# Tying sums of weight blocks to the split that precedes them, in a hybrid decoder step on one core

## The chip, the cores and the metric

One core of one Trainium2 chip runs the whole step: one prompt of 512 tokens with 16 meta tokens ahead of it, and eight sample tokens. The metric is the device time of one execution in microseconds. The kernel before took 2041.84 us, the median of three runs (2037.86 to 2042.74).

## What is computed

One layer: input projection, windowed attention beside causal pooling, output projection, layer norm, a SwiGLU block, layer norm. The change lies in the SwiGLU block, which is

```python
mix = jnp.einsum('bte,ed->btd', jnp.concatenate([attn_out, pool_out], -1), w_o)
h1 = layer_norm(DEEPNORM_ALPHA * h + mix, ln1_g, ln1_b)
a = jax.nn.silu(jnp.einsum('btd,df->btf', h1, w_gate)) * jnp.einsum('btd,df->btf', h1, w_up)
ff = jnp.einsum('btf,fd->btd', a, w_down)
return layer_norm(DEEPNORM_ALPHA * h1 + ff, ln2_g, ln2_b)
```

with D_MODEL = 2048 and D_FF = 5632, for 520 tokens (512 prompt, 8 sample) in float32.

## The kernel before

**Three matmuls per weight block.** Every float32 weight block s is split (L181 to L187) into a rounded part wh, written by ScalarE (L185, a cast), and a remainder wl = s - wh, written by VectorE (L186). I call these two instructions the cast and the split's low part. `products` (L189) then issues three matmuls per block of 128 rows: wh by the high part of the activations (L192), wh by their low part (L193), wl by their high part (L195). So TensorE can begin a product when the cast is there, and meets the low part at its third matmul.

**Seven products in the place of eight.** Gate, up and most of down are computed as 2 x 2 block products with seven multiplications each. Four of the seven multiply a sum or difference of weight blocks, which VectorE makes in place: product 7 of (0,0) - (1,0), product 6 of (1,1) - (1,0), product 5 of (1,0) + (0,0), product 3 of (0,1) - (1,0), where the later ones read what the earlier ones wrote to (1,0). Products 1, 2 and 4 multiply a loaded block. "Sum" below means one of these four instructions: L930 for gate and up (128 x 1024), L1160 for down (128 x 640).

**Gate and up.** One set is one column tile of gate or of up: seven products, each with two halves of four blocks (`Set`, L915). 22 gate sets and 22 up sets alternate (g0, u0, g1, ...). The wh and wl tiles of a half turn in rings of five; the loaded weights turn in a ring of five tiles. VectorE also adds the products' PSUM banks into the outputs (L985, L991, L998, L1001, L1004, L1007) and stages the activations for the next part (L1024 to L1054). In the bank names p1_g11 is the bank of gate set 11 that products 1, 6, 5 and 3 fill, p7_g11 that of 7 and 4, p2_g11 that of 2. The first two sets of each kind and the ten after them have product 1 (some product 2 too) done ahead; I call them the filled sets. Of these g1, g2, g3, g4 and g6 and the up sets beside them take part in what follows.

**Down.** 32 pairs (chunk c of 4, column pair j of 8), each a generator with seven products of five blocks, so 7 x 5 x 3 = 105 matmuls (`column_pair`, L1141). Its PSUM tile is tri{c}_{j}: bank 0 for products 7 and 4, bank 1 for 2, bank 2 for 1, 6, 5 and 3. The outer loop (L1197) interleaves two pairs: product 1 of a pair is written ahead of product 3 of the pair before. wh and wl turn in rings of four. The weights of a pair are two tiles of 640 KB in a ring of eight, so four pairs fit; `load_w` (L1126) for pair x+3 stands behind the last product of pair x-1, whose buffers it takes. VectorE adds the banks into the accumulators: L1167 behind product 7, L1172 behind 6, L1177 behind 5, L1180 behind 3.

**Who sets the order.** The program is written down in the order of the code, and a scheduler then lays out each engine's queue by priorities and by its own model of time, keeping only the dependencies. Casts, splits and sums get a raised priority (`tc.high_priority`), so a sum can be pulled far ahead of where the code has it. Each engine runs its queue in order.

Of the kernel before, what the change touches and what calls it, by code (L numbers as in the profile page):

```python
# [7 lines left out]
F32 = mybir.dt.float32  # L8
# [58 lines left out]
def hybrid_step(ctx, tc, xin, w_in, w_o, w_g, w_u, w_d, w_pool, par_d, cst_d, ident_d, ln2gb, kct_d, vc_d, hist_d,  # L67
                ck_d, cv_d, sp_d, yp, ys, nkp, nvp, npp, nks, nvs, nps):
    nc = tc.nc
# [68 lines left out]
    prio = [0]  # L138
# [42 lines left out]
    def split(s, name, lo=None):  # L181

        wh, wl = [sp[0].tile(list(s.shape), F32R, tag=t, bufs=sp[1]) for t in ("wh", "wl")]
        with tc.high_priority(prio[0]):
            nc.scalar.copy(wh, s)  # L185
            (lo or nc.vector).tensor_sub(wl, s, wh.bitcast(F32))  # L186
        return wh, wl  # L187

    def products(out, wh, wl, hi, lo, first, last, onto=False):  # L189

        for j, o in enumerate(out):
            nc.tensor.matmul(o, wh, hi[j], start=first, stop=False, skip_group_check=onto)  # L192
            nc.tensor.matmul(o, wh, lo[j], start=False, stop=False, skip_group_check=onto)  # L193
        for j, o in enumerate(out):
            nc.tensor.matmul(o, wl, hi[j], start=False, stop=last, skip_group_check=onto)  # L195

    def full_block(src, name, out, hi, lo, low=None, apart=False):


        def mm(w, g, js):  # L200
            for kk in range(4):
                k = g * 4 + kk
                sl = slice(kk * P, (kk + 1) * P)
                products([out[j] for j in js], w[0][:, sl], w[1][:, sl], [hi(k)[j] for j in js], [lo(k)[j] for j in js],
                         k == 0, k == KT - 1)

        js = list(range(len(out)))
        ws = []
        for h in range(2):
            raw = load_raw(src[:, h * 1024:(h + 1) * 1024], f"{name}_{h}")  # L210
            for g in range(2):
                ws.append(split(raw[:, g * 512:(g + 1) * 512], f"{name}_{h}{g}", low))
                mm(ws[-1], 2 * h + g, js[:1] if apart else js)
        if apart:
            for g in range(4):
                mm(ws[g], g, js[1:])
# [27 lines left out]
    with ExitStack() as sa:  # L244
# [149 lines left out]
        def kv_weights(g, blocks):  # L394
            kvw.setdefault(g, []).extend(split(kvr[g, i // 2][:, i % 2 * 512:i % 2 * 512 + 512], f"kv{g}{i}")
                                         for i in blocks)
# [254 lines left out]
        def pool_group(g, apart=False):  # L651

            raw = load_raw(w_pool[:, g * 512:(g + 1) * 512], f"pool{g}")
            wph, wpl = split(raw, f"pool{g}")
            kbs = [8 + 2 * g + m for m in range(2)]
            for kb in kbs:
                mixf[kb] = row_tile(f"mixf{kb}")
            for hs in ((0,), (1,)) if apart else ((0, 1),):
                for m, kb in enumerate(kbs):
                    out = [mm_tile(f"pm{g}_{m}_{h}")[:, :HN] for h in hs]  # L660
                    for k in range(2):
                        c = k * 256 + m * P
                        products(out, wph[:, c:c + P], wpl[:, c:c + P], [dd[2 * g + k][0][:, HALF[h]] for h in hs],
                                 [dd[2 * g + k][1][:, HALF[h]] for h in hs], k == 0, k == 1)
                    for h, o in zip(hs, out):
                        nc.scalar.activation(mixf[kb][:, HALF[h]], o, AF.Copy, scale=par[:, PSC + kb - 8:PSC + kb - 7])
                yield
# [132 lines left out]
    def slot(name, shape=(2, HN), at=None):  # L800
        return gp.tile([P, *shape], F32R, tag="g", name=name, bufs=NG, at=at)
# [3 lines left out]
    for h in range(2):  # L805
        for k2 in range(KT // 2):
            mh[h].append(slot(f"mh{h}_{k2}"))
            ml[h].append(slot(f"ml{h}_{k2}"))
            for kk in range(2):
                s = mixf[2 * k2 + kk][:, HALF[h]]  # L810
# [104 lines left out]
    class Set:  # L915
# [10 lines left out]
            return self.raw[r, c]  # L926

        def s(self, t, a, b, op):
            with tc.high_priority(prio[0]):
                op(self.q(*t), self.q(*a), self.q(*b))  # L930
            return self.q(*t)

        def prod(self, n, bk, first=True):
# [207 lines left out]
    def column_pair(c, j):  # L1141

        A = {(r, b): wd[c, j, r, b] for r in range(2) for b in range(2)}
        tri = ps.tile([P, 3, 512], F32, tag="tri", name=f"tri{c}_{j}", bufs=2)[:, :, :HN]
        ga, de, al = [tri[:, i, :] for i in range(3)]
        ac = acc4[j]
        if c == 0:
            for r in range(2):
                h = ac[:, 2 * r:2 * r + 2, :]
                nc.scalar.activation(h, h, AF.Copy, scale=ALPHA)  # L1150

        def prod(n, bk, src, first=True):
            wh, wl = split(src, f"d{c}_{j}_{n}")
            for k in range(KP):
                hi, lo = ops[c][n][k][:, 0, :], ops[c][n][k][:, 1, :]
                products([bk], wh[:, k, :], wl[:, k, :], [hi], [lo], k == 0 and first, k == KP - 1, True)

        def add(t, a, b, op):
            with tc.high_priority(prio[0]):
                op(A[t], A[a], A[b])  # L1160
            return A[t]


        prod(1, al, A[0, 0])
        yield
        prod(7, ga, add((1, 0), (0, 0), (1, 0), nc.vector.tensor_sub))
        nc.vector.tensor_add(ac[:, 1:3, :], ac[:, 1:3, :], tri[:, 0::2, :])  # L1167
        yield
        prod(2, de, A[0, 1])
        yield  # L1170
        prod(6, al, add((1, 0), (1, 1), (1, 0), nc.vector.tensor_sub), False)
        nc.vector.tensor_add(ac[:, 0, :], ac[:, 0, :], al)  # L1172
        yield
        prod(4, ga, A[1, 1], False)
        yield
        prod(5, al, add((0, 0), (1, 0), (0, 0), nc.vector.tensor_add), False)
        nc.vector.tensor_add(ac[:, 0:2, :], ac[:, 0:2, :], tri[:, 0::2, :])  # L1177
        yield
        prod(3, al, add((0, 1), (0, 1), (1, 0), nc.vector.tensor_sub), False)
        nc.vector.tensor_add(ac[:, 2:4, :], ac[:, 2:4, :], tri[:, 1:3, :])  # L1180
        yield
# [15 lines left out]
    for x, (c, j) in enumerate(pairs[2:], 2):  # L1197
# [5 lines left out]
        for i in range(5):  # L1203
# [7 lines left out]
            elif j == 0 and i == 0:  # L1211

                ah, al_ = [], []
                for f in range(2 * len(PLAIN)):
                    t = slot(f"af{f}", (NTOK,), 16 + f).bitcast(F32)
# [173 lines left out]
```

## Time and profile before

| | before |
|---|---|
| median of 3 runs | 2041.84 us |
| the profiled execution | 2042.2 us |
| its span, first to last instruction | 2040.4 us |
| TensorE busy | 1939.2 us, 95% |
| VectorE busy | 1534.8 us, 75% |
| ScalarE busy | 946.6 us, 46% |
| mean DMA rate | 156 GB/s |
| mean granted TensorE clock | 0.982 |

The span leaves out 1.8 us around the instructions. Gate and up fill most of the stretch from 600 to 1469 us, down that from 1469 to about 1966 us, of which 1500 to 1930 us holds nothing else; the rest is input projection, attention and output projection ahead, and the last products of two plain column tiles and the last layer norm behind. A row of the windows view gives the busy time of each engine in a stretch, in microseconds, then the granted clock, the DMA share and the rate. A row of the waits view says who waited for whom, how long in all, how often, and the longest.

### The profile page before, as it was taken

How to read it: one execution, taken by the hardware profiler on the slowest of the kernel's cores; microseconds unless marked ns; L12 is line 12 of the kernel's file. 1: busy time of each engine (PE TensorE's matmuls, PEld its weight loads, DVE VectorE, ACT ScalarE, POOL GpSimd, SP SyncE). 2: the span in 40 equal slices, each digit the busy share in tenths (PEclk: the TensorE clock that was granted, in tenths of full speed). 3: DMA queues.
4: the chain of work that ended last, by engine and by line, in shares of the span. 5: the costliest groups of instructions: out<-in, count | busy, mean ns of one | idle time of the engine just before them, and what ended most of it. 6: DMA issues, size and time to landing. Idle time of an engine off the chain costs nothing.

```text
span 2040.4 us, 39488 instructions
## 1 busy us (share of the span) xinstructions
PE 1939.2 (95%) x15571; PEld 1896.8 (93%) x15571; DVE 1534.8 (75%) x2730; ACT 946.6 (46%) x1805; POOL 2.5 (0%) x8
## 2 busy tenths in 40 slices
PE   8999999999999999999999999999998888888995
PEld 8999999999989999999999999999998888888895
DVE  6666667666678889888888888888876666666678
ACT  6643436446464444555555555555443333333331
POOL 0000000000000000000000000000000000000000
PEclk9999999999999999999999999999999999999998
DMA  8722223656564555444445444445785445353232
GB/s 261 232 84 78 73 79 101 205 183 209 170 195 151 169 182 172 143 164 135 152 146 166 135 162 144 158 136 186 254 293 193 139 149 192 125 183 111 71 94 84
DMA packets 144986, 319.27 MB, mean 156 GB/s; under 512 B 14160, under 2 KB 65944, under 8 KB 144696
## 3 DMA queue, kind: packets, MB, share of 16 engines
q1 hardware_dynamic: 143680, 314.65, 46.9%
q8 instruction: 122, 2.00, 0.4%
q10 hardware_dynamic: 1120, 2.10, 0.3%
q14 instruction: 64, 0.52, 0.1%
HBM read 265.20 MB, written 54.03 MB: 156 GB/s over the span
## 4 chain that ended last, share of the span: by engine, by line
PE 71%; DVE 12%; DMA 11%; issue 3%; ACT 2%; DVEq 0%; SPq 0%; ACTq 0%
DMA fr<-in_w_d_dram 6%; PE p_u L195 6%; PE p_u L192 6%; PE p_u L193 6%; DVE rr L186 5%; PE p_g L192 5%; PE p_g L193 5%; PE p_g L195 5%; PE tri L192 4%; PE tri L195 4%; PE tri L193 4%; PE o L192 3%; PE o L195 3%; PE o L193 3%; DMA fr<-in_w_u_dram 2%
## 5 line engine op out<-in xcount | busy, mean ns | idle before, releaser
L185 ACT CAST rr<-fr 128x512 fp32r<-128x512 f32 (+1 forms) x1056 | 664.7, 643 | 837.9 <-PE tri L193 226.1
L186 DVE TENSOR_TENSOR rr<-fr,rr 128x512 fp32r<-128x512 f32 (+1 forms) x1056 | 736.1, 717 | 210.4 <-ACT rr L185 204.5
L930 DVE TENSOR_TENSOR fr<-fr 128x1024 f32<-128x1024 f32 x176 | 215.3, 1224 | 63.2 <-DMA fr<-in_w_g_dram 34.3
L195 PE MATMUL tri<-rr 128*128 128x260 f32 x696 | 205.9, 296 | 37.4 <-DVE rr L186 36.3
L192 PE MATMUL p_g<-rr 128*128 128x260 f32 x800 | 227.1, 285 | 5.2 <-DVE fr L1001 5.2
L192 PE MATMUL p_u<-rr 128*128 128x260 f32 x800 | 226.2, 284 | 2.2 <-ACT rr L185 1.3
L195 PE MATMUL p_g<-rr 128*128 128x260 f32 x800 | 222.2, 282 | 1.3 <-DVE rr L186 1.3
L195 PE MATMUL p_u<-rr 128*128 128x260 f32 x800 | 222.3, 282 | 0.0
L193 PE MATMUL p_u<-rr 128*128 128x260 f32 x768 | 215.9, 282 | 0.0
L193 PE MATMUL p_g<-rr 128*128 128x260 f32 x768 | 215.8, 282 | 0.0
L192 PE MATMUL tri<-rr 128*128 128x260 f32 x696 | 204.4, 294 | 4.9 <-DVE fr L1177 1.8
L193 PE MATMUL tri<-rr 128*128 128x260 f32 x696 | 202.7, 291 | 0.0
L1160 DVE TENSOR_TENSOR fr<-fr 128x640 f32<-128x640 f32 x128 | 104.8, 822 | 102.5 <-DMA fr<-in_w_d_dram 102.3
L195 PEld LDWEIGHTS tri<-rr 128*128 128x128 f32 x696 | 137.7, 198 | 43.2 <-DVE rr L186 43.2
L192 PEld LDWEIGHTS p_g<-rr 128*128 128x128 f32 x800 | 150.6, 188 | 7.7 <-DVE fr L1001 7.3
L192 PEld LDWEIGHTS p_u<-rr 128*128 128x128 f32 x800 | 150.7, 188 | 3.6 <-ACT rr L185 1.9
L195 PEld LDWEIGHTS p_g<-rr 128*128 128x128 f32 x800 | 149.5, 189 | 1.5 <-DVE rr L186 1.5
L195 PEld LDWEIGHTS p_u<-rr 128*128 128x128 f32 x800 | 149.6, 189 | 0.0
L192 PE MATMUL o<-rr 128*128 128x260 f32 x512 | 146.0, 286 | 0.3 <-ACT rr L185 0.3
L193 PEld LDWEIGHTS p_u<-rr 128*128 128x128 f32 x768 | 144.3, 188 | 0.0
L193 PEld LDWEIGHTS p_g<-rr 128*128 128x128 f32 x768 | 144.3, 188 | 0.0
L195 PE MATMUL o<-rr 128*128 128x260 f32 x512 | 143.9, 283 | 0.2 <-DVE rr L186 0.2
(300 smaller groups left out, 4770.7 us busy)
## 6 DMA issues: line engine op xcount, KB each, us to landing
fr<-in_w_g_dram SPq DMA_DIRECT2D x95, 512.0 KB
fr<-in_w_u_dram SPq DMA_DIRECT2D x95, 512.0 KB
fr<-in_w_d_dram SPq DMA_DIRECT2D x64, 640.0 KB
t_d<-fr SPq DMA_DIRECT2D x140, 260.0 KB
fr<-in_w_o_dram SPq DMA_DIRECT2D x64, 512.0 KB
fr<-in_w_in_dram SPq DMA_DIRECT2D x46, 512.0 KB
rr<-t_d SPq DMA_DIRECT2D x87, 260.0 KB
mid_b<-t_d SPq DMA_DIRECT2D x53, 260.0 KB
```

The source lines that it names most:

```text
L185: nc.scalar.copy(wh, s)
L186: (lo or nc.vector).tensor_sub(wl, s, wh.bitcast(F32))
L192: nc.tensor.matmul(o, wh, hi[j], start=first, stop=False, skip_group_check=onto)
L193: nc.tensor.matmul(o, wh, lo[j], start=False, stop=False, skip_group_check=onto)
L195: nc.tensor.matmul(o, wl, hi[j], start=False, stop=last, skip_group_check=onto)
L930: op(self.q(*t), self.q(*a), self.q(*b))
L1160: op(A[t], A[a], A[b])
```

## The change

Each sum now carries a dependency on the low part of the split that was written down last before it, in the order of the code. The dependency is of order alone (no semaphore: both run on VectorE): it tells the scheduler that the sum may not stand ahead of that split in VectorE's queue. Nothing is computed otherwise, and the number of instructions of each kind stays.

```diff
         with tc.high_priority(prio[0]):
             nc.scalar.copy(wh, s)
-            (lo or nc.vector).tensor_sub(wl, s, wh.bitcast(F32))
+            last_lo[0] = (lo or nc.vector).tensor_sub(wl, s, wh.bitcast(F32)).ins
         return wh, wl
+
+    last_lo = [None]
+
+    def weight_sum(op, *args):
+
+        with tc.high_priority(prio[0]):
+            i = op(*args).ins
+        tc.add_manual_dep(i, last_lo[0].name, mybir.DependencyInfo(mybir.DependencyClass.NoSync,
+                                                                   mybir.DependencyReason.DATA), reason="sum")
...
         def s(self, t, a, b, op):
-            with tc.high_priority(prio[0]):
-                op(self.q(*t), self.q(*a), self.q(*b))
+            weight_sum(op, self.q(*t), self.q(*a), self.q(*b))
             return self.q(*t)
...
         def add(t, a, b, op):
-            with tc.high_priority(prio[0]):
-                op(A[t], A[a], A[b])
+            weight_sum(op, A[t], A[a], A[b])
             return A[t]
```

The nine new lines move the line numbers: a sum is L194 in the changed kernel, the matmuls are L201, L202 and L204, and the additions of banks stand 7 or 8 lines further down. The orders below are those of the queues; they hold no times.

VectorE's queue in down, from the addition behind product 6 of pair (2,2) on (tri2_2 is its PSUM tile, tri2_3 the next pair's). Before:

```order
L1172 TENSOR_TENSOR fr_60<-fr_60,tri2_2_18244 128x260
L186 TENSOR_TENSOR rr_61<-fr_60,rr_61 128x640
L1160 TENSOR_TENSOR fr_60<-fr_60 128x5x128
L186 TENSOR_TENSOR rr_61<-fr_60,rr_61 128x640
L1177 TENSOR_TENSOR fr_60<-fr_60,tri2_2_18244 128x520
L1160 TENSOR_TENSOR fr_60<-fr_60 128x5x128
L186 TENSOR_TENSOR rr_61<-fr_60,rr_61 128x640
L1160 TENSOR_TENSOR fr_60<-fr_60 128x5x128
L1167 TENSOR_TENSOR fr_60<-fr_60,tri2_3_18377 128x520
L1160 TENSOR_TENSOR fr_60<-fr_60 128x5x128
L186 TENSOR_TENSOR rr_61<-fr_60,rr_61 128x640
L1180 TENSOR_TENSOR fr_60<-fr_60,tri2_2_18244 128x520
```

Counted off against the code, the first L186 is the low part of product 3 of (2,2), and the first L1160 is the sum of product 7 of pair (2,5), three pairs ahead; the three others are the sums of products 6, 5 and 3 of (2,3). With the change the same place reads:

```order
L1179 TENSOR_TENSOR fr_60<-fr_60,tri2_2_18244 128x260
L186 TENSOR_TENSOR rr_61<-fr_60,rr_61 128x640 x2
L194 TENSOR_TENSOR fr_60<-fr_60 128x5x128
L186 TENSOR_TENSOR rr_61<-fr_60,rr_61 128x640
L1184 TENSOR_TENSOR fr_60<-fr_60,tri2_2_18244 128x520
L186 TENSOR_TENSOR rr_61<-fr_60,rr_61 128x640
L194 TENSOR_TENSOR fr_60<-fr_60 128x5x128
L1174 TENSOR_TENSOR fr_60<-fr_60,tri2_3_18377 128x520
L186 TENSOR_TENSOR rr_61<-fr_60,rr_61 128x640
L1187 TENSOR_TENSOR fr_60<-fr_60,tri2_2_18244 128x520
```

The first L194 is now the sum of product 7 of (2,3), the next pair, right ahead of its own split; no sum stands more than a few instructions ahead of the split that reads it. TensorE's order of products is the same in both from the third pair on.

VectorE's queue in gate set 11, from the addition of product 2 on. Before:

```order
L998 TENSOR_TENSOR fr_60<-p2_g11_10474,fr_60 128x260
L186 TENSOR_TENSOR rr_61<-fr_60,rr_61 128x512 x2
L930 TENSOR_TENSOR fr_60<-fr_60 128x1024
L1001 TENSOR_TENSOR fr_60<-fr_60,p1_g11_10373 128x260
L186 TENSOR_TENSOR rr_61<-fr_60,rr_61 128x512 x2
L1004 TENSOR_TENSOR fr_60<-fr_60,p7_g11_10404 128x260
```

With the change:

```order
L1006 TENSOR_TENSOR fr_60<-p2_g11_10474,fr_60 128x260
L186 TENSOR_TENSOR rr_61<-fr_60,rr_61 128x512 x2
L1009 TENSOR_TENSOR fr_60<-fr_60,p1_g11_10373 128x260
L186 TENSOR_TENSOR rr_61<-fr_60,rr_61 128x512 x2
L194 TENSOR_TENSOR fr_60<-fr_60 128x1024
L1012 TENSOR_TENSOR fr_60<-fr_60,p7_g11_10404 128x260
```

The sum is that of product 7 of the up set that follows (u11). It has moved from ahead of the addition of bank p1_g11 (L1001, now L1009) to behind it and behind the two splits of product 1 of u11.

TensorE's queue in gate set 3, one of the filled ones, where product 4 begins (bank p7_g3). Before:

```order
L192 MATMUL p2_g3_7456<-mid_b_3870,rr_61 128x260
L193 MATMUL p2_g3_7456<-mid_b_3870,rr_61 128x260
L195 MATMUL p2_g3_7456<-mid_b_3870,rr_61 128x260
L192 MATMUL p7_g3_7385<-rr_61 128x260
L193 MATMUL p7_g3_7385<-rr_61 128x260
L192 MATMUL p1_g3_7384<-rr_61 128x260
```

With the change:

```order
L201 MATMUL p1_g3_7384<-rr_61 128x260
L202 MATMUL p1_g3_7384<-rr_61 128x260
L204 MATMUL p1_g3_7384<-rr_61 128x260
L201 MATMUL p7_g3_7385<-rr_61 128x260
L202 MATMUL p7_g3_7385<-rr_61 128x260
L201 MATMUL p1_g3_7384<-rr_61 128x260
```

Before, product 2 (bank p2_g3) is the last ahead of product 4; now it is the second half of product 6 (bank p1_g3), and product 2 has come earlier. Gate sets 1, 2, 3, 4 and 6 are so.

## The prediction

> **What bounds the kernel now.** I read the page first, then windows by stage, then the waits of the stage that stands out, then the timeline of one of its pairs, then windows of 1 us for the clock. Page:
>
> ```profile
> span 2040.4 us, 39488 instructions
> PE 1939.2 (95%) x15571; PEld 1896.8 (93%) x15571; DVE 1534.8 (75%) x2730; ACT 946.6 (46%) x1805; POOL 2.5 (0%) x8
> ```
>
> TensorE is busy 95% of the span, but that is a mean over stages. The windows view for gate and up, for 10 us of the change to down, for all of down, and for 22 whole pairs in it (start and length, then busy time of PE, PEld, DVE, ACT and POOL, granted clock, DMA share, GB/s):
>
> ```profile
> 600.00:1469.00 869.00, 856.86 (x7075) 851.26 (x7073) 733.51 (x1156) 451.19 (x844) 0.00 (x0) 1.00 0.49 160
> 1480.00:1490.00 10.00, 10.00 (x86) 10.00 (x85) 5.71 (x8) 4.57 (x7) 0.00 (x0) 1.00 0.89 350
> 1500.00:1930.00 430.00, 376.49 (x2869) 366.55 (x2870) 290.43 (x414) 144.56 (x203) 0.00 (x0) 0.95 0.47 156
> 1555.89:1907.64 351.75, 304.50 (x2311) 296.06 (x2311) 234.63 (x335) 113.63 (x158) 0.00 (x0) 0.95 0.45 150
> ```
>
> Gate and up have TensorE busy for 98.6% of the time at full clock: little to win. Down has it idle for 53.5 of 430 us, at a granted clock of 0.95, with every other engine and the DMA further from full: there a wait is the bound. Who waits for whom in down (sum, times, longest):
>
> ```profile
> DVE fr L1160 <- DMA fr<-in_w_d_dram: 102.3, 24, 5.6
> PE tri L195 <- DVE rr L186: 41.0, 22, 2.8
> PE tri L192 <- DVE fr L1177: 7.3, 4, 3.5
> PE tri L192 <- DVE fr L1167: 4.2, 4, 1.8
> ```
>
> VectorE waits 24 times, once per pair, for a weight transfer, and only at the sum; TensorE waits 22 times for a low part. The timelines of one pair (start, length, instruction, and in brackets the idle time ahead of it with its releaser), sorted by time, show that it is one event:
>
> ```profile
> 1740.01 3.21 SPq L1133 DMA_DIRECT2D fr<-in_w_d_dram  x2
> 1741.27 0.73 ACT L185 CAST rr<-fr 128x640 fp32r<-128x640 f32 x1 [1.01 <-PE tri L193]
> 1742.04 0.83 DVE L186 TENSOR_TENSOR rr<-fr,rr 128x640 fp32r<-128x640 f32 x1 [0.21 <-ACT rr L185]
> 1742.98 0.28 PE L192 MATMUL tri<-rr 128*128 128x260 f32 x1
> 1746.56 0.28 PE L192 MATMUL tri<-rr 128*128 128x260 f32 x1
> 1746.96 0.82 DVE L1160 TENSOR_TENSOR fr<-fr 128x640 f32<-128x640 f32 x1 [4.10 <-DMA fr<-in_w_d_dram]
> 1747.70 0.82 DVE L186 TENSOR_TENSOR rr<-fr,rr 128x640 fp32r<-128x640 f32 x1
> 1748.57 0.38 PE L195 MATMUL tri<-rr 128*128 128x260 f32 x1 [1.62 <-DVE rr L186]
> ```
>
> The low part at 1742.04 ends at 1742.87 and is the last reader of two weight tiles; their next load moves from 1742.89 to 1746.87 (the chain of waits has it as its own step, below). The sum, next in VectorE's queue, needs that load, so VectorE stands for 4.10 us. Behind it is queued the low part of 1747.70, which starts as the sum ends, so its cast was ready; TensorE, at 1748.57, needs that one. Load, sum and low part are 3.98 + 0.82 + 0.82 us in a row against TensorE's lead. The queue in the section on the change says the same: the sum is that of the pair three ahead, and nothing needs it yet.
>
> **Part 1: the wait in down goes.** With the change the sum of product 7 of a pair stands right ahead of its own split, some three pairs after its load could begin. Two of the chain's rows give the length of the 22 pairs, and one the load:
>
> ```profile
> 1555.89 0.39 PE tri L195
> 1742.89 3.98 DMA fr<-in_w_d_dram
> 1907.64 0.39 PE tri L195
> ```
>
> Between the two matmuls, both right behind a stall, lie 351.75 us and 22 x 105 = 2310 matmuls, the 2311 of the window: 15.99 us a pair. Undisturbed matmuls, from 1742.98 to 1746.56, are 30 in 3.58 us: 0.1193 us each. So 2310 x 0.1193 = 275.6 us, 12.53 a pair, and 76.1 us are lost, 3.46 a pair: 47.3 as idle time (351.75 - 304.50), the other 28.9 at a lowered clock. Both go if the stall does: **-76.1**. The load has then 2 to 3 pairs, over 25 us, for its 4.
>
> Outside of these 22 pairs down idles 53.5 - 47.3 = 6.2 us more, partly behind the additions L1177 and L1167 (rows above), some of which were late behind a sum. I take half: **-3.1**.
>
> What is late next? VectorE's work for a pair, by groups of one shape between 600 and 1930 us (busy, mean ns | idle before):
>
> ```profile
> L186 DVE TENSOR_TENSOR rr<-fr,rr 128x640 fp32r<-128x640 f32 x210 | 169.0, 822 | 34.2 <-ACT rr L185 33.0 <-PE tri L195 0.3
> L1160 DVE TENSOR_TENSOR fr<-fr 128x640 f32<-128x640 f32 x122 | 99.9, 822 | 102.5 <-DMA fr<-in_w_d_dram 102.3
> L1167 DVE TENSOR_TENSOR fr<-fr,tri 128x520 f32<-128x520 f32 x30 | 20.8, 693 | 1.2 <-PE tri L195 1.2
> L1172 DVE TENSOR_TENSOR fr<-fr,tri 128x260 f32<-128x260 f32 x30 | 12.7, 425 | 5.6 <-PE tri L195 5.6
> ```
>
> Seven low parts, four sums, three additions of 520 columns (L1167, and L1177 and L1180 at the same price) and one of 260: 11 x 0.822 + 3 x 0.693 + 0.425 = 11.55 us, against TensorE's 12.53. VectorE fits, but at 92%, so order decides. A ring of four wh and wl lets a cast begin when the product four splits back has ended, and where TensorE then has just one product (15 matmuls, 1.79 us) ahead of it and meets the low part two matmuls later (0.24), the chain has 2.03 us. It takes, from the rows of the pair above, about 0.05 to the cast (as from the low part's end, 1748.52, to its matmul), 0.77 from its start to the low part's (1741.27 to 1742.04), and 0.87 from the start of the low part to its matmul (1747.70 to 1748.57): 1.7. The slack of 0.33 us is less than one more VectorE instruction. Followed by hand through the new queue, product 7 and product 1 of the next pair are the two with so short a lead in each pair, and both pass, since the sum of product 7 is done about 0.6 us before its buffer comes free. For jitter I take 0.2 us a pair over 27 pairs, an estimate between nothing and the 2 x (0.82 - 0.33) = 1.0 that one VectorE instruction in the way of both would cost: **+5.4**, with ends 0 and 27.
>
> Where does the clock come from? Windows of 1 us around the stall ahead of the one above (the digits behind the five engines are the clock, DMA share, GB/s):
>
> ```profile
> 1731.00:1732.00 1.00, 0.00 (x0) 0.00 (x0) 1.00 (x2) 0.00 (x0) 0.00 (x0) 1.00 0.63 243
> 1733.00:1734.00 1.00, 1.00 (x10) 1.00 (x10) 1.00 (x3) 0.01 (x1) 0.00 (x0) 0.95 0.00 0
> 1734.00:1735.00 1.00, 1.00 (x6) 1.00 (x6) 1.00 (x2) 0.72 (x1) 0.00 (x0) 0.50 0.00 0
> 1736.00:1737.00 1.00, 1.00 (x7) 1.00 (x7) 1.00 (x2) 0.21 (x1) 0.00 (x0) 0.50 0.00 0
> ```
>
> TensorE stands still through 1731 to 1732, works again, and gets half the clock from 1734 to 1737. At 1480 to 1490, with no idle time and twice the DMA traffic, the clock is 1.00. So I count the lowered clock as a consequence of the stalls. The Trainium skill, page "TensorE: Matmul & The Clock Gate", section "HAM oscillation — how this bites in real kernels", sets its rule at TensorE-idle gaps longer than about 3.4 us; the longest wait for a low part here is 2.8, so by it these stalls would not lower the clock, the cause would be another and would stay, as in the first rival. The trace disagrees: the 0.50 comes within 3 us of such a stall.
>
> **Part 2: gate and up.** TensorE's waits there:
>
> ```profile
> PE p_g L192 <- DVE fr L1001: 5.2, 8, 1.7
> PE p_u L195 <- DVE rr L186: 2.7, 4, 0.7
> PE p_g L195 <- DVE rr L186: 1.3, 1, 1.3
> PE p_u L192 <- ACT rr L185: 1.3, 3, 0.7
> PE p_u L192 <- DVE fr L1001: 0.9, 2, 0.5
> ```
>
> Together 11.4 us. Set 11 (timelines) shows the main kind:
>
> ```profile
> 994.76 1.23 DVE L930 TENSOR_TENSOR fr<-fr 128x1024 f32<-128x1024 f32 x1 [2.00 <-DMA fr<-in_w_u_dram]
> 995.90 0.42 DVE L1001 TENSOR_TENSOR fr<-fr,p_g 128x260 f32<-128x260 f32 x1
> 996.37 0.39 PE L192 MATMUL p_g<-rr 128*128 128x260 f32 x1 [0.61 <-DVE fr L1001]
> ```
>
> The sum waits for the up set's weights, and the addition that frees a PSUM bank waits behind it. The change puts the addition first, and takes sums from between casts and low parts: **-11.4**. In return gate sets 1, 2, 3, 4 and 6 get TensorE's new order (the second half of product 6 directly ahead of product 4), and the cast for product 4 takes the buffer that this half has just left. With no lead TensorE waits for a whole cast:
>
> ```profile
> L185 ACT CAST rr<-fr 128x512 fp32r<-128x512 f32 x586 | 353.2, 619 | 321.1 <-PE p_u L193 118.9 <-PE p_g L193 84.1 <-DVE fr L930 76.5
> ```
>
> 0.62 and about 0.05 on each side, say 0.75 us, five times: **+3.8** (0 if the other engines run later than I think). The stage nets -7.6; its ends are -11.4 and, if the old stalls only move, +3.8.
>
> **Sum**, against the profiled execution of 2042.2 us (the span and 1.8 around it; 0.4 above the median): 2042.2 - 76.1 - 3.1 + 5.4 - 7.6 = **1960.8, forecast 1961 us**. No instruction is added or removed, and no queue other than VectorE's and a few places of TensorE's and ScalarE's is moved.
>
> **The rivals.**
> *The clock stays low.* If down's 0.95 were due to load and not to stalls, 0.05 x 430 = 21.5 us would remain: 1982. Against it are the 1.00 at 1480 to 1490 and the 0.50 behind a stall. Chance 0.08.
> *The slack is eaten.* The upper end of the residue: a low part late by one VectorE instruction at both tight products of each pair, 27 us in the place of 5.4: 1982; with the clock lowered by it too, 2004. For it speaks VectorE's 92%; against it the order, walked by hand. Chance 0.20.
> *The wait only moves.* The first split that reads the load waits in the sum's place, and only gate and up gain: 2042.2 - 7.6 = 2035. Against it: the load is issued pairs ahead and takes 4 us, with DMA at 0.47. Chance 0.04.
> *The lost lead, slower.* Sums made early were ready when their cast came. Now the sum waits for the preceding low part, that one for its cast, that one for TensorE to free a buffer. If a sum ends after its buffer is free, sum, cast and low part stand in a row: 0.82 + 0.05 + 0.77 + 0.87 = 2.51 us of stall where nothing was hidden before. Over 3.46 / 2.51 = 1.4 such sums per pair the change loses; with two it is 2042.2 + (5.0 - 3.46) x 27 - 7.6 = 2076. Against it: the sum with the shortest lead is done 0.6 us early. Chance 0.05.
>
> **Numbers.** The forecast has 0.63, and gives 1961. Its own ends are 1948 (no residue, no new wait in gate and up, all of the 6.2) and 1974 (twice the residue, nothing won in gate and up). To reach 8 in 10 the range takes in the rivals at 1982 and, with the clock, 2004; below, the 2 us by which runs of a kernel scatter: 1946 to 2004. A difference of 0.3%, 6 us, is about what a measurement of this kernel can tell from no change. Faster 0.92, same 0.03 (a wait that only moves, with a little less gain than priced), slower 0.05.
>
> **What would show it.** Right: sums that wait for w_d loads almost gone (102.3 us before); 22 pairs of down in about 280 us at clock 1.00 with TensorE busy 98% and more; VectorE near 90% there; the waits for L1009 (the old L1001) gone; five waits of about 0.75 us for casts in gate sets 1 to 4 and 6. Wrong: pairs of over 13.2 us with TensorE waiting for low parts that follow a sum directly (lost lead, or slack eaten), a clock under 0.98 in down without stalls, or a load that the split now waits for.

## The result and the profile after

| | before | changed |
|---|---|---|
| median | 2041.94 us (4 runs) | 1976.12 us (4 runs, 1975.06 to 1978.68) |
| ratio | | 0.9683, 95% interval 0.9667 to 0.9700 |
| the profiled execution's span | 2040.4 us | 1974.6 us |
| mean granted clock | 0.982 | 0.987 |

The kernel is 65.8 us faster; the forecast was 81 us, 1961, and the measured time lies inside its range. The page of the changed kernel:

```profile
span 1974.6 us, 39350 instructions
PE 1916.5 (97%) x15571; PEld 1881.8 (95%) x15571; DVE 1545.2 (78%) x2730; ACT 936.6 (47%) x1805; POOL 2.5 (0%) x8
```

The page hides that the stages went opposite ways. The windows view shows it, for the first 300 us of gate and up and for 370 us of down. First the kernel before, then the changed one:

```profile
600.00:900.00 300.00, 293.01 (x2397) 289.68 (x2396) 261.45 (x426) 148.72 (x272) 0.00 (x0) 1.00 0.50 163
1530.00:1900.00 370.00, 321.44 (x2448) 312.40 (x2447) 248.61 (x355) 119.99 (x167) 0.00 (x0) 0.95 0.46 152
```

```profile
600.00:900.00 300.00, 278.38 (x2179) 271.46 (x2178) 244.22 (x393) 133.97 (x248) 0.00 (x0) 0.97 0.47 152
900.00:1400.00 500.00, 500.00 (x4172) 500.00 (x4172) 424.65 (x655) 263.01 (x510) 0.00 (x0) 1.00 0.46 149
1530.00:1900.00 370.00, 368.21 (x3061) 367.27 (x3060) 314.15 (x445) 151.70 (x215) 0.00 (x0) 1.00 0.52 178
```

The counts of matmuls in a stretch of fixed length are the shortest way to read such a change. Down gets 3061 in the place of 2448, TensorE 99.5% busy at full clock: 370 / 3061 x 105 = 12.69 us a pair, where I had forecast 12.53 and 0.2. The later sets of gate and up (900 to 1400 us) have no idle time left, and 4172 matmuls where the kernel before has 4128. But between 600 and 900 us, where the filled sets are, 218 matmuls fewer are done, 26 us at 0.1193. TensorE's waits of the changed kernel there, and those left in down (1530 to 1900 us):

```profile
PE p_g L201 <- ACT rr L185: 7.4, 10, 1.7
PE p_g L201 <- DVE fr L999: 6.7, 5, 1.4
PE p_g L201 <- DVE fr L1009: 4.1, 3, 2.9
PE p_g L204 <- DVE rr L186: 2.8, 6, 1.1
```

```profile
PE tri L204 <- DVE rr L186: 1.2, 1, 1.2
PE tri L201 <- DVE fr L1179: 0.6, 1, 0.6
```

In down two waits are left, 1.8 us together, where there had been one per pair. In the filled sets TensorE waits for casts and for additions of banks. Two of the prediction's signs did not come: VectorE is at 85% in down (314.15 of 370 us), not near 90, and three waits for L1009 (the old L1001) are left, though all ahead of 900 us.

### The profile page after: what moved, and what is told of

It is laid out like the page before. It is cut to its first block, busy times and chain, and to the rows that moved or that the text cites. A ratio compares the mean times of both kernels' runs of the same rounds, so it can differ in the third digit from the quotient of the medians.

```text
span 1974.6 us, 39350 instructions
## 1 busy us (share of the span) xinstructions
PE 1916.5 (97%) x15571; PEld 1881.8 (95%) x15571; DVE 1545.2 (78%) x2730; ACT 936.6 (47%) x1805; POOL 2.5 (0%) x8
## 4 chain that ended last, share of the span: by engine, by line
PE 58%; DVE 5%; DMA 2%; issue 1%; ACT 1%; DVEq 0%; ACTq 0%; SPq 0%
PE tri L201 7%; PE tri L204 7%; PE tri L202 7%; PE p_u L201 6%; PE p_u L202 6%; PE p_u L204 6%; PE p_g L201 6%; PE p_g L204 6%; PE p_g L202 6%; DMA fr<-in_w_g_dram 2%; DVE fr L194 2%; DVE rr L186 1%; PE d L204 1%; DMA t_d<-fr 1%; PE d L202 1%
## 5 line engine op out<-in xcount | busy, mean ns | idle before, releaser
L185 ACT CAST rr<-fr 128x512 fp32r<-128x512 f32 (+1 forms) x1056 | 655.6, 643 | 849.7 <-DVE fr L194 289.0
L186 DVE TENSOR_TENSOR rr<-fr,rr 128x512 fp32r<-128x512 f32 (+1 forms) x1056 | 733.4, 716 | 265.6 <-ACT rr L185 253.7
L194 DVE TENSOR_TENSOR fr<-fr 128x1024 f32<-128x1024 f32 (+1 forms) x304 | 319.3, 1050 | 37.3 <-DMA fr<-in_w_g_dram 21.7
L201 PE MATMUL p_g<-rr 128*128 128x260 f32 x800 | 231.2, 290 | 15.9 <-DVE fr L999 6.7
L204 PE MATMUL p_g<-rr 128*128 128x260 f32 x800 | 225.8, 287 | 1.1 <-DVE rr L186 1.1
L201 PE MATMUL p_u<-rr 128*128 128x260 f32 x800 | 225.5, 283 | 0.0
L204 PE MATMUL p_u<-rr 128*128 128x260 f32 x800 | 222.0, 282 | 0.0
L202 PE MATMUL p_g<-rr 128*128 128x260 f32 x768 | 219.6, 287 | 0.0
L202 PE MATMUL p_u<-rr 128*128 128x260 f32 x768 | 216.0, 282 | 0.0
L204 PE MATMUL tri<-rr 128*128 128x260 f32 x696 | 196.8, 283 | 1.2 <-DVE rr L186 1.2
L201 PE MATMUL tri<-rr 128*128 128x260 f32 x696 | 197.1, 283 | 0.8 <-ACT rr L185 0.8
L202 PE MATMUL tri<-rr 128*128 128x260 f32 x696 | 196.7, 283 | 0.0
L201 PEld LDWEIGHTS p_g<-rr 128*128 128x128 f32 x800 | 154.2, 193 | 19.9 <-DVE fr L999 7.7
L204 PEld LDWEIGHTS p_g<-rr 128*128 128x128 f32 x800 | 153.3, 193 | 1.4 <-DVE rr L186 1.3
L201 PEld LDWEIGHTS p_u<-rr 128*128 128x128 f32 x800 | 150.6, 188 | 0.0
L204 PEld LDWEIGHTS p_u<-rr 128*128 128x128 f32 x800 | 149.7, 189 | 0.0
L202 PEld LDWEIGHTS p_g<-rr 128*128 128x128 f32 x768 | 148.0, 193 | 0.0
L201 PE MATMUL o<-rr 128*128 128x260 f32 x512 | 146.0, 286 | 0.3 <-ACT rr L185 0.3
L202 PEld LDWEIGHTS p_u<-rr 128*128 128x128 f32 x768 | 144.3, 188 | 0.0
L204 PE MATMUL o<-rr 128*128 128x260 f32 x512 | 143.9, 283 | 0.2 <-DVE rr L186 0.2
L202 PE MATMUL o<-rr 128*128 128x260 f32 x512 | 144.0, 282 | 0.0
L204 PEld LDWEIGHTS tri<-rr 128*128 128x128 f32 x696 | 131.3, 189 | 1.7 <-DVE rr L186 1.4
```

Of the source, the lines that this page charges most:

```text
L186: last_lo[0] = (lo or nc.vector).tensor_sub(wl, s, wh.bitcast(F32)).ins
L194: i = op(*args).ins
```

## The experiments

My theory after the result was that the loss in the filled sets comes from TensorE's new order around product 2, and that down's gain stands by itself. The rivals were that the parts depend on each other, or that tied sums are late everywhere. All experiments are edits of the changed kernel, but for one of the kernel before. "Untied" means that a sum is issued as before the change.

### Each part alone

`down_only` unties the sums of gate and up, `gateup_only` those of down (the diff is that of `down_only`; the other does the same to `add` in down):

```diff
-            weight_sum(op, self.q(*t), self.q(*a), self.q(*b))
+            with tc.high_priority(prio[0]):
+                op(self.q(*t), self.q(*a), self.q(*b))
```

> Sums tied in down alone; gate and up as before. Theory (the two parts add up, and down's gain stands by itself): the traces have the stretch from the first matmul of down to the end 84.9 us shorter with the change (548.57 to 463.65), and the stretch ahead of it 19.1 us longer (1469.11 to 1488.20); so 2041.9 - 84.9 = 1957, with the sum of product 7 not waiting for loads and the pair at 12.5 us. Rival (the later start of down, or its fuller buffers, is part of the gain): down keeps some of its waits, above 1962. Rival (what gate and up lost comes with the ties in down too): about 1976.

> Sums tied in gate and up alone; down as before. Theory: 2041.9 + 19.1 = 2061, slower than before, with TensorE's waits behind the addition of product 6 (1.4 us each, five) and the casts of product 4 (0.6 each, five) in the filled gate sets, and down's waits for loads back at about 100 us. Forecast as it stood in the prediction: a gain of 7.6 us, 2034. Rival (gate and up lose only because down's loads reach into them): within 5 us of before.

Measured: 1956.75 us (ratio 0.9576, 0.9553 to 0.9599) and 2063.13 us (1.0094, 1.0071 to 1.0116). The first is 85.2 us faster than before, the second 21.2 slower; together -64.0, and the whole change has -65.8. The parts add up: down gains more than forecast, and the half in gate and up loses.

### Where in gate and up

By the code, `filled` holds for ten sets: g1, g2, g3, g4, g6 and the up sets beside them. The section on the kernel before counts "the first two sets of each kind" to them as well; it is one of each kind, g0 and u0, and they are not `filled` here but the first sets. `unfilled_down` keeps the tie in down and in unfilled sets; `late_sets` drops it in the first sets too:

```diff
+            filled = self.filled = self.p1 is not None
+            Set.seen = Set.seen or filled
...
-            weight_sum(op, self.q(*t), self.q(*a), self.q(*b))
+            if not (self.seen and not self.filled):
+                with tc.high_priority(prio[0]):
+                    op(self.q(*t), self.q(*a), self.q(*b))
+            else:
+                weight_sum(op, self.q(*t), self.q(*a), self.q(*b))
```

(The diff is that of `late_sets`; `unfilled_down` asks for `self.filled` alone.)

> Sums tied in down and in the unfilled sets of gate and up; the filled sets as before, with TensorE's order of before. Theory (all of the loss of gate and up lies in the filled sets, the unfilled ones gain the 4 to 5 us of their stalls behind the old L1001): 2041.9 - 84.9 - 4.5 = 1952 to 1953, 23 to 24 us under the changed kernel, and 4 to 5 under a tie in down alone. Rival (a tie costs lead in every set): not under the tie in down alone, 1957 or more.

> Sums tied in down and in those unfilled sets of gate and up alone that come after the filled ones; the first gate and up set and the filled ones as before. In the run with all unfilled sets tied, TensorE still stood for 2.84, 0.38, 0.22, 1.70, 0.59 and 1.62 us between 610 and 652 us (7.4 in all, 2 more by a lowered clock), where the tie in down alone has 2.4. Theory (the tie costs where VectorE and the loads have no slack, at the start and in the filled sets, and gains behind them): 1956 - 7 = 1949, the fastest so far. Rival (the later sets gain nothing): 1957, as the tie in down alone.

Measured: 1955.92 us (0.9569, 0.9545 to 0.9592), which can't be told from `down_only`, so the expected 4 to 5 us weren't there; and 1947.50 us (0.9539, 0.9517 to 0.9560), near the 1949 expected. The intervals of the two, and those of `late_sets` and `down_only`, just overlap, but the matmuls by stage agree with the theory: from 600 to 660 us `late_sets` does 456 and `unfilled_down` 400; from 900 to 1400 us `late_sets` does 4172 and `down_only` 4128. So the tie costs time in the first sets and in the filled ones, and gains some in those behind them.

### What is lost in the filled sets

`hold_two` leaves all sums tied and puts product 2 back behind product 6 on TensorE:

```diff
+            i = nc.tensor.matmul(o, wh, hi[j], start=first, stop=False, skip_group_check=onto).ins
+            if hold[0] is not None:
+                tc.add_manual_dep(i, hold[0].name, mybir.DependencyInfo(mybir.DependencyClass.NoSync,
+                                                                        mybir.DependencyReason.DATA), reason="hold")
+                hold[0] = None
...
+                hold[0] = last_mm[0] if filled else None
                 self.prod(2, de)
```

> The changed kernel, with the first matmul of product 2 tied behind the last of product 6 in the filled sets (an order on TensorE's own queue; nothing else is changed): 24 matmuls, 2.86 us, stand again between product 6 and product 5, which reuses its bank. Theory (the loss is TensorE's order, product 2 ahead of the end of product 6, which leaves two matmuls ahead of the bank's next use): the five waits of 1.4 for the addition and the five of 0.6 for product 4's cast go, with the lowered clock that follows (about 1.8 each): 5 x 3.8 = 19 us, 1957 or somewhat above. Rival (VectorE is late in these sets because of the sums themselves and the staging beside them): the waits come back elsewhere in the set, above 1970.

Measured: 1992.22 us (0.9745, 0.9721 to 0.9769), 16 us slower than the change itself. The waits for the addition of product 6 (L999, now L1005) are gone, but larger ones stand elsewhere. TensorE's waits in the same 300 us, first rows:

```profile
PE p_g L208 <- DVE rr L186: 14.3, 10, 2.5
PE p_g L201 <- ACT rr L185: 6.8, 8, 1.7
PE p_u L201 <- ACT rr L185: 3.8, 4, 1.5
PE p_u L208 <- DVE rr L186: 3.7, 8, 2.1
```

So my theory fell: TensorE's order decided where the wait shows, not that there is one. What VectorE itself waited for between 655 and 815 us said more: before, changed, and `hold_two`, the rows of loads:

```profile
DVE fr L930 <- DMA fr<-in_w_g_dram: 4.4, 5, 1.4
```

```profile
DVE fr L194 <- DMA fr<-in_w_g_dram: 13.9, 4, 4.1
```

```profile
DVE fr L194 <- DMA fr<-in_w_u_dram: 13.1, 4, 3.9
DVE fr L194 <- DMA fr<-in_w_g_dram: 10.3, 4, 3.7
```

It is a wait of the kind that the change takes away in down, made anew in the filled sets. One of them in the changed kernel (the sums in VectorE's timeline and SyncE's issues of weight loads, sorted by time), then the same place before:

```profile
706.97 0.35 SPq L178 DMA_DIRECT2D fr<-in_w_g_dram  x1
708.61 1.22 DVE L194 TENSOR_TENSOR fr<-fr 128x1024 f32<-128x1024 f32 x1
708.72 0.35 SPq L178 DMA_DIRECT2D fr<-in_w_g_dram  x1
709.86 0.33 SPq L178 DMA_DIRECT2D fr<-in_w_g_dram  x1
715.73 1.23 DVE L194 TENSOR_TENSOR fr<-fr 128x1024 f32<-128x1024 f32 x1 [3.17 <-DMA fr<-in_w_g_dram]
```

```profile
695.64 1.22 DVE L930 TENSOR_TENSOR fr<-fr 128x1024 f32<-128x1024 f32 x1
696.93 0.34 SPq L178 DMA_DIRECT2D fr<-in_w_g_dram  x1
698.09 0.35 SPq L178 DMA_DIRECT2D fr<-in_w_g_dram  x1
699.03 0.33 SPq L178 DMA_DIRECT2D fr<-in_w_g_dram  x1
701.58 1.22 DVE L930 TENSOR_TENSOR fr<-fr 128x1024 f32<-128x1024 f32 x1 [1.30 <-DMA fr<-in_w_g_dram]
```

In each, the first sum is that of product 3 of the up set. It is, by the code, the last reader of the tile that held (1,0), and 0.03 to 0.07 us after its end the load that takes this place is issued, which product 7 of the next gate set needs; the last row is that product's sum. With the tie the sum of product 3 can't be done early: its load goes out last of three, where it was the first before. New theory: the tie of this one sum delays the loads; the ring of five tiles has no room to take that up, as I think because a filled set leaves product 1 out and so is shorter (no run varies the ring). Between 702 and 706 us, just ahead of it, nothing is transferred at all (length, engines, then clock, DMA share, GB/s):

```profile
702.00:706.00 4.00, 4.00 (x35) 4.00 (x35) 3.21 (x6) 1.94 (x4) 0.00 (x0) 1.00 0.00 0
```

The chain of work that ended last, in the changed kernel, goes through this load and through four others like it between 668 and 840 us; the sum ahead of it, the load and the sum behind it:

```profile
708.69 1.14 DVE fr L194
709.86 5.85 DMA fr<-in_w_g_dram
715.73 1.23 DVE fr L194
```

Three kernels test it. `tie_765` unties product 3's sum in gate and up, `tie_3` ties only that one (`t == (0, 1)`), `no_load` ties all but gives filled sets no loads, so that their products are of what the tiles held:

```diff
-            weight_sum(op, self.q(*t), self.q(*a), self.q(*b))
+            if t != (0, 1):
+                weight_sum(op, self.q(*t), self.q(*a), self.q(*b))
+            else:
+                with tc.high_priority(prio[0]):
+                    op(self.q(*t), self.q(*a), self.q(*b))
```

```diff
-        with tc.high_priority(prio[0]):
-            nc.sync.dma_start(raw, src)
+        if not stale:
+            with tc.high_priority(prio[0]):
+                nc.sync.dma_start(raw, src)
```

> The changed kernel, but the sum of product 3 of the gate and up sets is not tied. That sum is the last reader of the tile that held (1,0), whose place the next set's weights take. New theory (with the tie that sum comes later, the loads of the next set start later, and its first sum stands in VectorE's queue for them: 13.9 us of such waits between 655 and 815 us, 4.4 before): the waits fall to about 5 us in that stretch and most of the 23 us lost comes back, 1955 to 1962. Old theory (TensorE's order around product 2, which returns here as well): the same. Rival (every tied sum costs lead; product 3's is one in four): three quarters of the loss stay, about 1971.

> Sums tied in down, and in gate and up that of product 3 alone. Theory (it is this sum, the last reader of the tile whose place the next set's weights take, whose tie costs the time): the loss of the full tie comes back, 1970 or more, with VectorE's waits for w_g or w_u at the sums in the stretch from 655 us at 10 us or more. Rival (the loss comes from all four sums being late): about a quarter of it, 1957 to 1963.

> The changed kernel with all its ties, but the filled sets load no weights (their products are of what the tiles held). Theory (what the tie costs there is VectorE's waiting for loads that start late): without loads the loss goes although every sum is tied: 1950 to 1958. Rival (tied sums are late for their splits whether or not there are loads; VectorE is nearly full in these sets): the waits of TensorE stay, above 1968.

Measured: `tie_765` 1942.21 us (0.9513, 0.9491 to 0.9534), better than expected and the fastest of all; `tie_3` 1979.24 us (0.9707, 0.9688 to 0.9725), the whole loss from one sum in four; `no_load` 1950.62 us (0.9553, 0.9531 to 0.9574), with every sum tied. VectorE's waits from 655 to 815 us, of `tie_765` (all its rows) and the first of `tie_3`:

```profile
DVE fr L1066 <- DMA t_d<-fr: 4.7, 4, 1.4
DVE rr L186 <- ACT rr L185: 3.3, 7, 0.6
```

```profile
DVE fr L942 <- DMA fr<-in_w_g_dram: 10.6, 4, 3.4
```

And 600 to 900 us of `tie_765`, 2467 matmuls to the 2179 of the change and the 2397 of before, then of `no_load`:

```profile
600.00:900.00 300.00, 297.86 (x2467) 296.51 (x2466) 271.57 (x440) 154.13 (x285) 0.00 (x0) 1.00 0.51 167
600.00:900.00 300.00, 292.68 (x2406) 290.16 (x2405) 265.24 (x428) 147.12 (x275) 0.00 (x0) 1.00 0.28 93
```

The new theory holds. By their traces `tie_765` and `no_load` also bring TensorE's old order back in the filled gate sets (product 2 the last ahead of product 4), while `tie_3` has that of the change in most of them. So neither of the two sets the order aside; `hold_two` does. It has the old order too, and more than the whole loss; from `no_load`, with all sums tied in both, it differs in the gate sets mainly by the loads: 1992 and 1951 us. That `no_load` stays 8 us over `tie_765` leaves some room for tied sums that are late without any load, and no run without ties and without loads was made, so what leaving out the loads gains by itself is not known.

### What the wait in down was

`down_noprio` is the kernel before, without ties, its sums in down not raised in priority:

```diff
-            with tc.high_priority(prio[0]):
-                op(A[t], A[a], A[b])
+            op(A[t], A[a], A[b])
```

> The kernel before without any tie, but the sums of down are not given the raised priority. In VectorE's queue the sum of product 7 then stands right ahead of its own split, as with the tie; TensorE's order of products is that of before. Theory (down lost its time to that sum's wait for its load, ahead of splits that TensorE needed): as with the tie in down alone, 1957, 2 or 3 more where a sum comes too late. Rival (the gain needs the few products of TensorE that the tie moved, or the other sums' places): 1975 or more.

Measured: 2040.55 us (1.0003, 0.9987 to 1.0018), no change. The expectation had misread the queue: the sum that stands ahead of the low part of product 7 there is still that of the pair three ahead. VectorE's waits for the loads, 1500 to 1930 us:

```profile
DVE fr L1159 <- DMA fr<-in_w_d_dram: 102.1, 24, 6.0
```

The wait stayed, and the time with it. It also shows that the raised priority of the sums, to which the words on the kernel before point, is not what puts that sum so early in down. I take it to be the scheduler's model of time, which no run shows.

`down_seven` ties in down only the sum of product 7, `down_not_seven` (with `!=`) only the other three; gate and up are untied in both:

```diff
+            if (t, a) == ((1, 0), (0, 0)):
+                weight_sum(op, A[t], A[a], A[b])
+            else:
+                with tc.high_priority(prio[0]):
+                    op(A[t], A[a], A[b])
```

> In down only the sum of product 7 is tied; gate and up as before. It is the one sum that VectorE waited for a load at. Theory: the whole gain of down comes from it, as with all of down's sums tied, 1957. Rival (the sums of 6, 5 and 3 also stood ahead of low parts that TensorE waited for): part of the stalls stays, 1965 or more.

> The other way about: in down the sums of products 6, 5 and 3 are tied, that of 7 is not and stands three pairs ahead of its split in VectorE's queue, now ahead of product 2's low part. Theory: VectorE's waits for the loads stay, some 4 us a pair, and with them most of the loss: 2020 to 2045. Rival (the ties of the others, or the changed places of the splits, hide the wait): under 2000.

Measured: 1984.97 us (0.9725, 0.9709 to 0.9741) and 2010.21 us (0.9846, 0.9825 to 0.9867). Neither theory was met: the first came out by its rival, the second between the two. Of the 85 us, 57 come with the tie of product 7 alone and 31 with the other three alone. TensorE's waits from 1520 to 1900 us in `down_seven`, then, in `down_not_seven`, VectorE's for loads and the largest of TensorE's:

```profile
PE tri L201 <- DVE fr L1179: 14.3, 25, 0.6
PE tri L204 <- DVE rr L186: 1.9, 1, 1.9
```

```profile
DVE fr L1172 <- DMA fr<-in_w_d_dram: 35.0, 20, 3.2
PE tri L201 <- ACT rr L185: 34.2, 19, 3.3
```

With the load's wait gone, TensorE waits in `down_seven` in nearly every pair for L1179, there the addition behind product 7, which frees a bank. By VectorE's timeline two untied sums stand between product 7's low part and it, by their order those of products 6 and 5; with all sums tied it is one. This wait was hidden behind the larger one. In `down_not_seven` VectorE's waits for loads fell too, to 35.0 us from the 97.3 of the kernel before in this stretch. So its 31 us are not those of the other sums' places alone: where these stand also sets how long the untied sum waits.

`late_cast_1` makes the cast of product 7 twice in each pair, to measure the slack:

```diff
+            for _ in range(late[0]):
+                nc.scalar.copy(wh, s)
             nc.scalar.copy(wh, s)
```

> The changed kernel with the cast of product 7 made twice in each pair of down from the third on (0.73 us more on ScalarE ahead of the low part; the same numbers result). TensorE's order of products is the same. By the prediction's slack of 0.33 us TensorE would wait about 0.65 - 0.33 = 0.3 us a pair, with 30 pairs 9 to 10 us: 1985 or more. By the trace of the changed kernel, where low parts of product 7 and of product 1 end some 0.5 us ahead of their matmuls, 0.1 us a pair: 1976 to 1980.

Measured: 1995.76 us (0.9778, 0.9764 to 0.9793), 19.6 us more than the change, 0.65 for each of 30 pairs. The two casts of one pair (L186 is the added one, L187 the cast, L188 the low part in this kernel), then TensorE's timeline at this wait, and at that of the next pair:

```profile
1715.55 0.73 ACT L186 CAST rr<-fr 128x640 fp32r<-128x640 f32 x1 [2.33 <-PE tri L205]
1716.31 0.73 ACT L187 CAST rr<-fr 128x640 fp32r<-128x640 f32 x1
1717.33 0.28 PE L205 MATMUL tri<-rr 128*128 128x260 f32 x1
1717.96 0.39 PE L207 MATMUL tri<-rr 128*128 128x260 f32 x1 [0.35 <-DVE rr L188]
1718.18 0.28 PE L204 MATMUL tri<-rr 128*128 128x260 f32 x1
```

```profile
1731.22 0.39 PE L207 MATMUL tri<-rr 128*128 128x260 f32 x1 [0.33 <-DVE rr L188]
```

The wait shown, 0.33 to 0.35 us, looks like the 0.3 expected, but it is not the delay. The row counts the idle time from the modelled end of the matmul ahead, 0.28 us after its start, where undisturbed matmuls follow each other in 0.12: from 1717.33 to 1717.96 are 0.63 us, 0.51 too many, and the next one is 0.10 late again. That makes 0.61 us a pair; from one wait to the next are 13.26 us, where most pairs of the changed kernel take 12.54 to 12.66. The added cast moved the chain by 0.76 us (1715.55 to 1716.31), and 0.51 of it reached TensorE: the slack is 0.25 us here, not 0.33.

## Why the prediction was right in the sum, and where it failed

**The wait in down (-76.1, -3.1, +5.4; together -73.8).** The mechanism was right, the size too small: the tie in down alone gives -85.2. The residue of 5.4 isn't there, since two waits of 1.8 us together are all that is left in 370 us, and of the 6.2 us idle outside the 22 pairs nearly all goes, not half (1.3 us are left in the same stretch). These two make -82; the last 3 us I have not traced. The 28.9 us that the prediction put down to a lowered clock are not all that: a clock of 0.95 over 351.75 us loses 17.6, and some of the rest must be idle time that the busy time hides, as in `late_cast_1`. The sum doesn't depend on how the 76.1 is split. What I had not seen is that two causes lay one on the other: I took the late load for the whole 3.46 us a pair, and by `down_seven` taking its sum away brings two thirds; the other sums' places would have kept a third.

**The slack** of 0.33 us was near, 0.25 by `late_cast_1`, and neither "the slack is eaten" nor "the lost lead" came in the changed kernel. But one ScalarE instruction more brings the first about, and at 0.65 us a time, about twice what the wait's own row shows. VectorE had more room than the 92% worked out from recorded lengths: it is 85% busy, since instructions recorded with 0.82 us follow each other in 0.74 (1746.96 and 1747.70 in the prediction's timeline).

**The clock** in down is 1.00, as the part on it said; the rival that it stays low is refuted. So is "the wait only moves" as it was written, for down. A wait of its kind arose in gate and up, where I had not looked for it, and by `gateup_only` it doesn't need the tie in down.

**Gate and up (-11.4 + 3.8 = -7.6)** is the step that failed: it is +21. The five waits of the casts for product 4 came as forecast, 0.59 us each in the place of 0.75. But the step priced only what TensorE's order does to casts and splits. It did not ask when the sums release what they read, although the same question, what a load waits for, was the core of Part 1. The sum of product 3 gates the next set's load, and the ring of five tiles had no time to spare. It also overlooked, in the order fence that it rests on, that bank p1 is used again two matmuls after product 6 ends; that is where TensorE then stood for 1.0 to 1.4 us. The -11.4 itself was there to be had: untying one sum in four gives 1942.2, 14.5 below `down_only`, and the intervals of the two ratios don't meet.

That the time lies within the range is in part luck. Down came out 11 us better than its three terms and gate and up 29 us worse; a miss of +29 alone would have given 1990, still inside a range that had been widened for other rivals.

## What to carry to other kernels

An operation in an in-order queue that is done earlier than needed can hold up what stands behind it, when its input is late; one that is done later than before holds up whoever takes the place of what it reads. So tie each by what it waits for and by what it releases: the best of the kernels run here ties all sums but that of product 3 in gate and up, whose end starts a load. And compare matmul counts by stage before trusting a total: here -66 in the place of -81 hides -85 and +21.

## What the runs showed of the hardware

The lowered clock came without a single long wait. In the changed kernel two short ones within 2 us are followed by matmuls of 0.42 in the place of 0.28 us for 3 us, four times over; one of them, with a row of the windows view (granted clock 0.50):

```profile
686.96 0.39 PE L201 MATMUL p_g<-rr 128*128 128x260 f32 x1 [0.59 <-ACT rr L185]
688.90 0.39 PE L201 MATMUL p_g<-rr 128*128 128x260 f32 x1 [1.44 <-DVE fr L999]
690.28 0.42 PE L202 MATMUL p_g<-rr 128*128 128x260 f32 x1
```

```profile
691.00:692.00 1.00, 1.00 (x6) 1.00 (x6) 0.40 (x1) 0.56 (x2) 0.00 (x0) 0.50 0.66 170
```

The Trainium skill, page "TensorE: Matmul & The Clock Gate", section "HAM oscillation — how this bites in real kernels", puts the limit at idle gaps of more than about 3.4 us; here the lowered clock followed 0.59 and 1.44. It did not follow every such pair: 0.59 and 1.01 (648.44 and 649.96 us) were followed by no lowered clock. And a wait that the profile shows as 0.34 us cost some 0.65 us of time.
